# Hybrid encoder trunk: 64-row logit products padded to 128 rows, and dilated units that divide before they transpose

## The chip, the cores and the metric

The kernel runs on one core of one Trainium2 chip. The metric is the device time of one execution in microseconds (us). TensorE (PE below; PEld is its weight load) multiplies matrices, VectorE (DVE) and ScalarE (ACT) work on tiles of 128 partitions, GpSimd (POOL) does a few small powers, and SyncE (SP) issues the transfers.

## The reference

Input `x` is 512 positions by 1024 channels, float32; the output has the same shape. Two layers run, each on the residual `x`:

```
x = x + 1/2 * SwiGLU_1(rms(x))
u = rms(x);  p = u @ W_in
   A: Fourier mixing, 8 channel groups x 128
   B: dilated window attention, 3 head groups (dilation 1, 4, 16) x 2 heads of 64 channels;
      the groups of a head slot share one softmax denominator
   C: differential attention, 4 heads, two softmax maps of 64 channels each, a = p0 - lambda * p1
   a position bias is added to the logits of B and C
x = x + (sum over A, B, C of sigmoid gate * branch output) @ W_out
x = x + 1/2 * SwiGLU_2(rms(x))
```

A final RMSNorm follows. In B and C a logit is the product of a query and a key of 64 channels, scaled by 1/8, plus a bias; each row of logits goes through a softmax and is multiplied with the values.

## The kernel before, in words

**Number format.** Large products are made in parts. A float32 operand is split into `hi` (its float32r rounding, made by ACT) and `lo` (the remainder, made by DVE); `mm3` (line 186) makes a product as three passes, lo x hi, hi x lo and hi x hi. A pass is one weight load and one matmul of up to 128 rows (the channels that are summed over), 128 columns of weights and up to 512 columns of the moving operand. In the trace all passes have the line of the helper `mm` (183), so they are told apart by the names of their tiles; the engine helpers give DVE and ACT instructions line 124.

**Order of the work.** Each engine runs its instructions in program order. Weight chunks (`Op`, pushed to `ops`) are the dense work: load by SP, split by ACT and DVE, and some 24 passes each. Attention units are generators, the chains. `run` keeps two dilated or four differential units in flight; `step` advances a chain that is expected to be ready and otherwise emits the next step of dense work. What is expected is the `Estimate` (lines 94 to 127): each pass adds its given us to TensorE's time, each DVE and ACT instruction a fixed part and a part per column. Those figures decide the order of emission and nothing else.

**Logits.** `stack_query` (585) puts the hi part of a head's (or map's) 64 channels on its own half of the 128 rows and the lo part on the other half. `stack_key` (591) makes `kh`, the hi part of the key of both halves, and `k2`, in which map m has lo on its own half and hi on the other. `stacked` (601) then needs two passes instead of three: one of 128 rows, which holds both mixed products, and one of 64 rows, hi x hi:

```
        mm(ps, q2[:, m, cols], k2[:, m], True, False, 0.216)
        mm(ps, q2[HALF[m], m, cols], kh[HALF[m]], False, True, 0.216)
```

In the trace the first is `acc<-pr,pr 128*128 128x512` and the second `acc<-kh,pr 64*128 64x512`. A call of `stacked` is called a pair below.

**Dilated units** (`dilated_unit`, 733 on): 8 in a layer (2 head slots x 4 residues of the position). Each makes a pair for the first group, then two 64-row products in plain float32 of `q12` and `k12` for the other two groups (two passes each in the trace), a negated, biased minimum and the exponentials (`ta` of 512 columns, `tb_` of 256, with their sums), the sum's reciprocal `z`, and `dg`, the identity times `z` (line 756). Six products of 128x128 blocks with `dg` (lines 760 to 763) transpose and divide at once; in float32 each is two passes. The blocks are copied from PSUM and multiplied with the values.

**Differential units** (`diff_unit`): 16 in a layer (4 heads x 4 blocks of 128 queries). Each makes two pairs, one for each map; DVE takes bias and minimum (`mx`), ACT the exponential; DVE scales the first map by its reciprocal sum and adds the second (`ta<-ta,z,ta`). Four `T.transpose` with the identity (line 849) follow, one pass each, and after two blocks the product with the values.

**Between them.** After the Fourier groups, the dilated units are emitted among the products of the Fourier branch; the keys and queries of the differential heads follow, and the differential units run among the gate products and those of the dilated branch. PSUM has 8 tiles (`acc`) for everything; a tile is free again when DVE or ACT has read it. `kh` has two buffers.

Of the kernel before, what the change touches and what calls it, by code (L numbers as in the profile page):

```python
# [16 lines left out]
P = 128  # L17
# [18 lines left out]

# Columns of the one-hot tables: diff heads, dilation 1, 4, 16.
OH_DIFF, OH_D1, OH_D4, OH_D16, OH_N = 0, 1024, 2048, 2304, 2560
# [14 lines left out]
def _onehot():  # L53
    """[33, OH_N]: column -> one-hot bucket of a relative position; row 32 marks masked ones."""
    oh = np.zeros((BUCKETS + 1, OH_N), np.float32)

    def put(col, rel, valid):
        if valid:
            oh[int(_bucket(np.array(rel))), col] = 1.0
        else:  # L60
            oh[BUCKETS, col] = 1.0

    for i in range(1023):
        put(OH_DIFF + i, i - 511, True)
        put(OH_D1 + i, i - 511, abs(i - 511) <= 64)
    for i in range(255):
        put(OH_D4 + i, 4 * (i - 127), abs(i - 127) <= 64)
        put(OH_D16 + i, 4 * (i - 127), (i - 127) % 4 == 0)
    return oh


def _dft():
    """Channel table [128, C|S] with the scale of the transform, and position tables [2, 128, 512].

    Position table par acts on the sums (par 0) or negated differences (par 1) of the two halves of
    the positions; its 256 columns for each of two row blocks are cos and sin of output 2 j + par,
    j < 128. The column of sin 0 holds cos of output 256 instead."""
    c = np.arange(P)
# [15 lines left out]
class Estimate:  # L94
    """Expected times, in us, that choose the order of emission: `time` is TensorE's, `ready` that of
    the last result of the chain being emitted."""

# [11 lines left out]
class _Engine:  # L109
    """An engine whose instructions are added up in the estimate."""  # L110

# [18 lines left out]
def encoder_kernel(ctx: ExitStack, tc: tile.TileContext, I: dict, out: bass.AP):  # L130
# [13 lines left out]

# [1 line left out]
    # Engines run their instructions in program order. Latency-bound chains are generators; dense  # L146
    # matmul work is emitted between their steps, as much as they are expected to wait.
    est = Estimate()
# [37 lines left out]
    def mm3(ps, w, xx, start, stop, us=0.216):  # L186
        """ps += w.T @ xx of (hi, lo) pairs."""
        mm(ps, w[1], xx[0], start, False, us)
        mm(ps, w[0], xx[1], False, False, us)
        mm(ps, w[0], xx[0], False, stop, us)  # L190

    class Op:
        """A weight chunk and the generator that uses it."""

# [4 lines left out]
        def load(self, parts=1):  # L199
            """Loads part after part, then splits part after part."""  # L200
            n = self.nb * P
# [31 lines left out]
    def advance(c):  # L233
        """The next step of a chain; it yields the wait beyond its own last result."""
        est.ready = c[0]
        try:
            wait = next(c[1])
            c[0] = est.ready + wait
        except StopIteration:
            chains.remove(c)  # L240
# [52 lines left out]
    def project(ps, w, xs, k0=0, first=True, last=True):  # L293
        """ps (+)= sum over k of w[k].T @ xs[k], a step for each k"""
        for k in range(len(xs)):
            mm3(ps, wk(w, k0 + k), xs[k], first and k == 0, last and k == len(xs) - 1)
            yield

# [1 line left out]
    vecs = cpool.tile([P, I["vecs"].shape[1]], F32, name="vecs")  # L300
# [9 lines left out]
    halfb = cpool.tile([P, DEPTH * 24], F32, name="halfb")  # L310
    # Cosines of the channel transform, in float32.
    cosf = cpool.tile([P, P], F32, name="cosf")
# [5 lines left out]

# [1 line left out]
    def rstd_cols(sq, scale, eps, tag):  # L320
        """[128, 4] of (scale * column sums of sq + eps) ** -0.5 (column c: positions 128 c ...)."""
        ss = acc()
# [11 lines left out]
    def diagonals(cols):  # L334
        """The diagonal matrices of cols, in two parts."""
        n = cols.shape[1]
# [10 lines left out]
    def bcast(dg, n=NTB):  # L347
        """PSUM [128, n * 128]: every row is the column sums of dg."""
        ps = acc()
# [4 lines left out]
    class Norm:  # L354
        """rms statistics of x, gathered block by block, and x * gain as float32r pairs."""

# [40 lines left out]
        def then(self, act):  # L397
            """act() as soon as the statistics are there"""
            def wait():
# [9 lines left out]
    class LastNorm:  # L409
        """The last norm, with its output, for each half of the positions."""  # L410

# [29 lines left out]

# [1 line left out]
    def ffn(l, which, norm, nxt):  # L443
# [63 lines left out]

# [1 line left out]
    skewed = []  # L509

    def bias_tables():
# [13 lines left out]
        for head in range(10):  # L525
# [3 lines left out]
            sk = dram.tile([P, pitch], F32, name=f"skew{head}")  # L529
            # Row p of sk is the head's vector moved by step_ * p.  # L530
            nc.sync.dma_start(
# [5 lines left out]
    def toeplitz(dst, head, base, n):  # L537
        """dst[p, j] = bias vector of the head at base - step_ * p + j"""
        nc.sync.dma_start(dst, skewed[head][:, base:base + n])

# [1 line left out]
    def token_major(l, norm, name, n, evict):  # L542
        """u @ the n columns of a weight, rows on partitions: one PSUM tile for each 128 positions."""
        ps = []
# [21 lines left out]
    def feature_tile(l, norm, t, scale, use):  # L566
        """use(rows of u @ W_in's columns of tile t, times scale)"""
        def body(w):
# [11 lines left out]

    # Logits of 64 channels: both mixed products of the parts in one pass of 128 rows. Of the two
    # heads (or maps) of a tile, m sits on rows 64 m ...; its other part lies on the other half.
    HALF = (slice(0, 64), slice(64, 128))

    def stack_query(view, q2, src):
        for m in range(2):
            own, other = HALF[m], HALF[1 - m]
            A.activation(view(q2[own, m]), src[own], AF.Copy)
            V.tensor_tensor(view(q2[other, m]), src[own], view(f(q2[own, m])), op=ALU.subtract)

    def stack_key(src):
        kh = tpool.tile([P, 512], F32R, tag="kh", name=nm("kh"), bufs=2)
        k2 = pair()
        A.activation(kh, src, AF.Copy)
        for m in range(2):
            own, other = HALF[m], HALF[1 - m]
            V.tensor_tensor(k2[own, m], src[own], f(kh[own]), op=ALU.subtract)
            A.activation(k2[other, m], src[own], AF.Copy)
        return kh, k2

    def stacked(ps, q2, cols, key, m):
        kh, k2 = key
        mm(ps, q2[:, m, cols], k2[:, m], True, False, 0.216)
        mm(ps, q2[HALF[m], m, cols], kh[HALF[m]], False, True, 0.216)

    def by4(ap):
        return ap.rearrange("p (u r) -> p r u", r=4)

    # Fourier mixing. The position transform of real rows gives cosine and sine sums, which are even
    # and odd in the output position s: Y[k, s] = P - Q and Y[k, 512 - s] = P + Q with  # L610
    # P = C Zcos, Q = S Zsin.
    def fourier_tables():
# [13 lines left out]
    def fold(norm, eo):  # L626
        """Sums and negated differences of the two halves of the positions."""
        def evict(ps):
# [46 lines left out]

    # Dilated attention: a joint softmax over the three groups of a head slot, for the queries of
    # one residue mod 4. The first group sees all keys (masked), the others those of the residue.
    def dilated_inputs(l, norm):
# [54 lines left out]
    def dilated_unit(d, po, s, r, bias):  # L733
# [20 lines left out]
        V.reciprocal(z, z)  # L754
        dg = spool.tile([P, P], F32, tag="dg", name=nm("dg"), bufs=2)
        V.tensor_scalar(dg, ident, z, None, op0=ALU.mult)
        yield 0.1
        # Transposes that divide by the sum.
        qa, qb_ = acc(), acc()
        for c in range(4):  # L760
            mm(qa[:, c * P:(c + 1) * P], ta[:, c * P:(c + 1) * P], dg, True, True, 0.216)
        for g in range(2):
            mm(qb_[:, g * P:(g + 1) * P], tb_[:, g * P:(g + 1) * P], dg, True, True, 0.216)
        pa, pb = tma(), tma()
# [7 lines left out]

    # Differential attention.
    def diff_inputs(l, norm):
        lam_init = 0.8 - 0.6 * math.exp(-0.3 * l)
        d = {"vc": [], "y": [None] * NDIFF}
        # -lambda on every partition
        lq = tma()
# [106 lines left out]
    def gate(l, norm, b, o, use):  # L885
        """use(tanh of half the gate's argument): 2 sigmoid(z) = 1 + tanh(z / 2)"""
        def body(w):
# [11 lines left out]
    def branch(src, nb, ys, use):  # L899
        """use(branch output)"""  # L900
        def body(w):
# [152 lines left out]
def _tiles(w):  # L1054
    """[L, K, N] -> [L, N/128, 128, K]: for each 128 columns, rows of 128 by row blocks."""
    L, K, N = w.shape
    return w.reshape(L, K // P, P, N // P, P).transpose(0, 3, 2, 1, 4).reshape(L, N // P, P, K)
# [54 lines left out]
```

## Time and profile before

| | |
|---|---|
| time, median of 3 runs | 2505.75 us (2504.47 to 2506.02) |
| span of the profiled execution | 2505.5 us |
| mean granted TensorE clock | 0.996 of full speed |
| PE / PEld busy | 2486.9 / 2051.9 us |
| DVE / ACT / POOL busy | 1263.0 / 900.9 / 16.4 us |
| DMA | 241.06 MB, 96 GB/s on average |

The profile is of one execution; the runs were timed separately, and no other time is given for the profiled one than its span, from the first to the last instruction. A matmul's end is modelled and passes overlap, so the distance from one start to the next, not the duration, tells what a pass costs. `xN` is the number of instructions that a row stands for. "issue" as the end of an idle time means that the engine waited for nothing that the profile shows.

### The profile page before, as it was taken

How to read it: one execution, taken by the hardware profiler on the slowest of the kernel's cores; microseconds unless marked ns; L12 is line 12 of the kernel's file. 1: busy time of each engine (PE TensorE's matmuls, PEld its weight loads, DVE VectorE, ACT ScalarE, POOL GpSimd, SP SyncE). 2: the span in 40 equal slices, each digit the busy share in tenths (PEclk: the TensorE clock that was granted, in tenths of full speed). 3: DMA queues.
4: the chain of work that ended last, by engine and by line, in shares of the span. 5: the costliest groups of instructions: out<-in, count | busy, mean ns of one | idle time of the engine just before them, and what ended most of it. 6: DMA issues, size and time to landing. Idle time of an engine off the chain costs nothing.

```text
span 2505.5 us, 28932 instructions
## 1 busy us (share of the span) xinstructions
PE 2486.9 (99%) x11618; PEld 2051.9 (82%) x11618; DVE 1263.0 (50%) x1961; ACT 900.9 (36%) x1335; POOL 16.4 (1%) x20
## 2 busy tenths in 40 slices
PE   8999999999999999999999999999999999999998
PEld 6788889887778888888888888888877788888888
DVE  5434454534775654344444344445367656443446
ACT  4222233534443332223332233344344444322234
POOL 0000000000000000000000000000000000000000
PEclk9999999999999999999999999999999999999999
DMA  4533232312222322332332323333122223223335
GB/s 155 154 93 106 91 101 93 96 57 75 94 72 81 115 93 90 96 104 88 103 101 80 114 93 88 100 100 98 50 85 77 79 71 114 93 85 109 99 95 160
DMA packets 82486, 241.06 MB, mean 96 GB/s; under 512 B 9305, under 2 KB 17241, under 8 KB 82352
## 3 DMA queue, kind: packets, MB, share of 16 engines
q1 hardware_dynamic: 82352, 239.22, 31.2%
q8 instruction: 91, 1.49, 0.2%
q14 instruction: 43, 0.35, 0.0%
HBM read 235.93 MB, written 6.91 MB: 97 GB/s over the span
## 4 chain that ended last, share of the span: by engine, by line
PE 99%; DVE 0%; DMA 0%; ACT 0%; issue 0%; POOL 0%; SPq 0%; POOLq 0%; DVEq 0%
PE acc L183 98%; PE acc L849 1%; DMA x<-in_xT 0%; DVE pr L124 0%; POOL srr L124 0%; ACT xs L124 0%; DVE xs L124 0%; DMA out<-t 0%; DVE t L124 0%; DVE wlo L124 0%; DVE sum L124 0%; SPq L1017 0%; SPq L205 0%; POOLq L1107 0%; ACT ch L124 0%
## 5 line engine op out<-in xcount | busy, mean ns | idle before, releaser
L183 PE MATMUL acc<-xs,whi 128*128 128x512 f32 x4032 | 1246.9, 390 | 0.3 <-DVE xs L124 0.3
L124 ACT ACTIVATE whi<-raw 128x1024 fp32r<-128x1024 f32 (+3 forms) x495 | 463.2, 936 | 1244.8 <-PE acc L183 740.7
L183 PEld LDWEIGHTS acc<-xs,whi 128*128 128x128 f32 x4032 | 759.1, 188 | 158.3 <-DVE xs L124 1.7
L183 PE MATMUL acc<-xs,wlo 128*128 128x512 f32 x2016 | 794.1, 394 | 7.4 <-ACT xs L124 5.7
L124 DVE TENSOR_TENSOR wlo<-raw,whi 128x1024 fp32r<-128x1024 f32 (+3 forms) x495 | 528.6, 1068 | 372.9 <-ACT whi L124 371.4
L183 PE MATMUL acc<-pr,whi 128*128 128x512 f32 (+1 forms) x2256 | 650.3, 373 | 0.0
L183 PEld LDWEIGHTS acc<-pr,whi 128*128 128x128 f32 x2256 | 412.1, 188 | 74.1 <-DVE pr L124 0.5
L183 PEld LDWEIGHTS acc<-xs,wlo 128*128 128x128 f32 x2016 | 379.9, 188 | 95.2 <-issue 9.6
L183 PE MATMUL acc<-pr,wlo 128*128 128x512 f32 (+1 forms) x1128 | 422.6, 375 | 0.0
L124 DVE TENSOR_TENSOR t<-acc,rows 128x512 f32<-128x512 f32 x238 | 163.8, 691 | 507.6 <-PE acc L183 505.5
L183 PEld LDWEIGHTS acc<-pr,wlo 128*128 128x128 f32 x1128 | 212.4, 188 | 38.1 <-issue 0.3
L183 PE MATMUL acc<-whi,xs 128*128 128x512 f32 (+1 forms) x512 | 153.6, 376 | 0.0
L124 ACT ACTIVATE pr<-t 128x512 fp32r<-128x512 f32 (+2 forms) x152 | 101.8, 670 | 56.3 <-DVE t L124 55.7
L124 DVE SCALAR_TENSOR_TENSOR x<-acc,x 128x512 f32<-128x512 f32 (+1 forms) x88 | 56.6, 643 | 127.2 <-PE acc L183 127.2
L183 PE MATMUL acc<-pr,pr 128*128 128x256 f32 (+2 forms) x624 | 112.8, 310 | 0.0
L183 PEld LDWEIGHTS acc<-whi,xs 128*128 128x128 f32 x512 | 95.3, 188 | 15.0
L183 PEld LDWEIGHTS acc<-pr,pr 128*128 128x128 f32 (+1 forms) x624 | 86.3, 190 | 17.6 <-issue 9.9
L183 PE MATMUL acc<-wlo,xs 128*128 128x512 f32 (+1 forms) x256 | 96.1, 375 | 0.0
L124 DVE TENSOR_TENSOR pr<-t,pr 128x512 fp32r<-128x512 f32 (+1 forms) x124 | 86.4, 697 | 6.2 <-ACT pr L124 5.6
L124 ACT ACTIVATE pr<-acc 128x512 fp32r<-128x512 f32 (+1 forms) x66 | 39.7, 608 | 80.4 <-PE acc L183 56.0
L124 DVE CUSTOM_DVE_ANT_0 ta<-acc,pr 128x512 f32<-128x512 f32 x80 | 54.4, 689 | 28.1 <-PE acc L183 27.4
L124 DVE TENSOR_TENSOR t<-t,t 128x512 f32<-128x512 f32 x88 | 60.9, 692 | 10.2 <-ACT t L124 1.3
(90 smaller groups left out, 1028.5 us busy)
## 6 DMA issues: line engine op xcount, KB each, us to landing
raw<-in_w_ffn_up SPq DMA_DIRECT2D x88, 512.0 KB
raw<-in_w_ffn_gate SPq DMA_DIRECT2D x87, 512.0 KB
raw<-in_w_ffn_down SPq DMA_DIRECT2D x72, 384.0 KB
raw<-in_w_gate SPq DMA_DIRECT2D x48, 512.0 KB
raw<-in_w_ffn_down SPq DMA_DIRECT2D x72, 320.0 KB
raw<-in_w_in SPq DMA_DIRECT2D x28, 512.0 KB
raw<-in_w_a SPq DMA_DIRECT2D x16, 512.0 KB
raw<-in_w_br_a SPq DMA_DIRECT2D x16, 512.0 KB
```

Source lines behind the costliest of these rows:

```text
L124: return call(out, *args, **kwargs)
L183: T.matmul(ps, w, xx, start=start, stop=stop)
L849: T.transpose(tr[:, c * P:(c + 1) * P], es[0][:, c * P:(c + 1) * P], ident)
```

## The change

The second pass of a pair takes all 128 rows. Two key tiles `kz`, made once, hold for each map the hi part on its own half of the rows and zeros on the other; the zeros are written by POOL at the start, and `stack_key` writes only the own halves, for each map with a copy of 64 rows. The weights of the pass are the whole of `q2[:, m]`, whose other half meets the zeros. The estimate of both passes goes from 0.216 to 0.228.

In a dilated unit DVE multiplies `ta` and `tb_` with `z` in place, and six transposes with the identity take the place of the six products with `dg`; their estimate goes from 0.216 to 0.109 each.

The program's scratch for dynamic DMA is made smaller. Comments and docstrings go as well, which moves no instruction.

```
--- before.py
+++ after.py
@@ -588,27 +588,37 @@
             A.activation(view(q2[own, m]), src[own], AF.Copy)
             V.tensor_tensor(view(q2[other, m]), src[own], view(f(q2[own, m])), op=ALU.subtract)
 
+    kzs = deque()
+    for i in range(2):
+        kz = cpool.tile([P, 2, 512], F32R, name=f"kz{i}")
+        for m in range(2):
+            nc.gpsimd.memset(f(kz[HALF[1 - m], m]), 0.0)
+        kzs.append(kz)
+
     def stack_key(src):
-        kh = tpool.tile([P, 512], F32R, tag="kh", name=nm("kh"), bufs=2)
+        kz = kzs[0]
+        kzs.rotate(1)
         k2 = pair()
-        A.activation(kh, src, AF.Copy)
         for m in range(2):
             own, other = HALF[m], HALF[1 - m]
-            V.tensor_tensor(k2[own, m], src[own], f(kh[own]), op=ALU.subtract)
+            A.activation(kz[own, m], src[own], AF.Copy)
+            V.tensor_tensor(k2[own, m], src[own], f(kz[own, m]), op=ALU.subtract)
             A.activation(k2[other, m], src[own], AF.Copy)
-        return kh, k2
+        return kz, k2
 
     def stacked(ps, q2, cols, key, m):
-        kh, k2 = key
-        mm(ps, q2[:, m, cols], k2[:, m], True, False, 0.216)
-        mm(ps, q2[HALF[m], m, cols], kh[HALF[m]], False, True, 0.216)
+        kz, k2 = key
+        mm(ps, q2[:, m, cols], k2[:, m], True, False, 0.228)
+        mm(ps, q2[:, m, cols], kz[:, m], False, True, 0.228)
 
@@ -752,15 +762,16 @@
         z = small(1, "z")
         V.tensor_add(z, s2[:, 0:1], s2[:, 1:2])
         V.reciprocal(z, z)
-        dg = spool.tile([P, P], F32, tag="dg", name=nm("dg"), bufs=2)
-        V.tensor_scalar(dg, ident, z, None, op0=ALU.mult)
+        V.tensor_scalar(ta, ta, z, None, op0=ALU.mult)
+        V.tensor_scalar(tb_[:, :256], tb_[:, :256], z, None, op0=ALU.mult)
         yield 0.1
         qa, qb_ = acc(), acc()
         for c in range(4):
-            mm(qa[:, c * P:(c + 1) * P], ta[:, c * P:(c + 1) * P], dg, True, True, 0.216)
+            T.transpose(qa[:, c * P:(c + 1) * P], ta[:, c * P:(c + 1) * P], ident)
+            est.pe(0.109)
         for g in range(2):
-            mm(qb_[:, g * P:(g + 1) * P], tb_[:, g * P:(g + 1) * P], dg, True, True, 0.216)
+            T.transpose(qb_[:, g * P:(g + 1) * P], tb_[:, g * P:(g + 1) * P], ident)
+            est.pe(0.109)
         pa, pb = tma(), tma()
         A.activation(pa, qa, AF.Copy)
         V.tensor_copy(pb[:, :256], qb_[:, :256])
@@ -1098,7 +1109,7 @@
-    nc = bacc.Bacc("TRN2", target_bir_lowering=False, num_devices=1)
+    nc = bacc.Bacc("TRN2", target_bir_lowering=False, num_devices=1, dynamic_dma_scratch_size=1024)
```

## Rows read from the trace of the kernel before

**Rows 1.** The page's busy line: us, share of the span and instructions of each engine.

```profile
PE 2486.9 (99%) x11618; PEld 2051.9 (82%) x11618; DVE 1263.0 (50%) x1961; ACT 900.9 (36%) x1335; POOL 16.4 (1%) x20
```

**Rows 2.** Groups by shape: count | busy us, mean ns of one | idle before, releasers.

```profile
L183 PE MATMUL acc<-kh,pr 64*128 64x512 f32 x80 | 41.5, 519 | 0.0
...
L183 PE MATMUL acc<-dg,ta 128*128 128x128 f32 x192 | 24.3, 278 | 0.0
...
L124 DVE TENSOR_SCALAR ta<-ta,z 128x512 f32<-128x512 f32 x32 | 15.3, 480 | 0.0
L183 PEld LDWEIGHTS acc<-kh,pr 64*128 64x128 f32 x80 | 15.2, 190 | 21.8 <-issue 21.8
...
L124 ACT ACTIVATE pr<-t 64x512 fp32r<-64x512 f32 x40 | 27.1, 676 | 0.6
...
L124 DVE TENSOR_SCALAR dg<-ident,z 128x128 f32<-128x128 f32 x16 | 4.6, 287 | 0.5
```

**Rows 3.** Timeline of PE, 606 to 620: start us, us, engine, line, operation, names, shape, count.

```profile
606.01 0.39 PE L183 MATMUL acc<-xs,wlo 128*128 128x512 f32 x1
...
608.05 0.39 PE L183 MATMUL acc<-pr,pr 128*128 128x512 f32 x1
608.37 0.50 PE L183 MATMUL acc<-kh,pr 64*128 64x512 f32 x1
...
612.22 0.58 PE L183 MATMUL acc<-pr,pr 128*128 128x512 f32 x1
...
616.35 0.79 PE L183 MATMUL acc<-xs,wlo 128*128 128x512 f32 x1
...
619.43 0.63 PE L183 MATMUL acc<-xs,whi 128*128 128x512 f32 x2
```

**Rows 4.** Stretches: bounds and length, busy us (instructions) of each engine, PEclk, DMA share, GB/s.

```profile
612.50:619.30 6.80, 6.80 (x13) 3.80 (x13) 4.72 (x17) 4.41 (x11) 0.00 (x0) 0.50 0.00 0
619.30:710.00 90.70, 90.70 (x416) 70.77 (x415) 65.93 (x126) 41.19 (x73) 1.01 (x1) 1.00 0.26 83
1848.00:1855.00 7.00, 7.00 (x14) 3.82 (x14) 4.68 (x17) 4.63 (x11) 0.00 (x0) 0.51 0.00 0
```

**Rows 5.** Timeline of PE, 64 to 70, the bias tables' products.

```profile
65.75 0.61 PE L183 MATMUL acc<-xs,whi 128*128 128x512 f32 x2
66.30 1.02 PE L183 MATMUL acc<-ta,rel 33*10 33x512 f32 x2
```

**Rows 6.** Timeline of PE, 547 to 549, a dilated unit's logits.

```profile
547.52 0.50 PE L183 MATMUL acc<-pr,pr 128*128 128x512 f32 x1
547.95 0.49 PE L183 MATMUL acc<-kh,pr 64*128 64x512 f32 x1
548.29 0.60 PE L183 MATMUL acc<-pr,pr 64*128 64x128 f32 x4
```

**Rows 7.** Timeline of PE, 508 to 518 and 630 to 632, transposes.

```profile
511.01 2.84 PE L183 MATMUL acc<-dg,ta 128*128 128x128 f32 x24
...
513.92 0.63 PE L183 MATMUL acc<-pr,whi 128*128 128x512 f32 x2
...
630.80 0.60 PE L849 MATMUL acc<-ident,ta 128*128 128x128 f32 x4
...
631.47 0.63 PE L183 MATMUL acc<-xs,whi 128*128 128x512 f32 x2
```

**Rows 8.** Timeline of DVE, 606 to 622, two of the differential units' reductions.

```profile
608.91 0.69 DVE L124 CUSTOM_DVE_ANT_0 ta<-acc,pr 128x512 f32<-128x512 f32 x1
...
609.75 0.69 DVE L124 CUSTOM_DVE_ANT_0 ta<-acc,pr 128x512 f32<-128x512 f32 x1
```

**Rows 9.** Waits of PE's weight loads: us in total, times, longest us.

```profile
PEld acc L183 <- DVE mx L124: 1.5, 6, 0.2
```

**Rows 10.** Timeline of all engines, 547 to 553: a diagonal and the transposes that use it.

```profile
550.12 0.29 DVE L124 TENSOR_SCALAR dg<-ident,z 128x128 f32<-128x128 f32 x1
...
550.99 1.50 PE L183 MATMUL acc<-dg,ta 128*128 128x128 f32 x12
```

## The prediction

> **What bounds the kernel now.** I read the page's busy line first: TensorE (PE) is busy 99% of the span, VectorE (DVE) 50%, ScalarE (ACT) 36% [rows 1]. So only time on PE's own queue counts, and the question is which of its steps are longer than they need be. A start-to-start step is what a pass costs; durations overlap and mislead. The groups by shape gave the candidates: 80 passes named `acc<-kh,pr` of 64 rows, before each of which the weight load sat idle for "issue" [rows 2]. The PE timeline prices them: the nine steps of ordinary 128-row passes from 606.01 to 608.05 take 0.227 us each, but from 608.37 on, where passes of 128 and of 64 rows alternate, the nine steps to 612.22 take 0.428 us each [rows 3]. Nothing else was waited for. The same pause stands where a 33-row pass of the bias tables follows a 128-row one: 66.30 is 0.32 us after the pass before it (the second of the pair that starts at 65.75), not 0.227 [rows 5]. So the height of the pass is the cause, not the operand: going from one height to another, the next weights are not loaded ahead. Last, the stretches: from 612.5 to 619.3 and around 1850 the granted clock is 0.50 (1.2 GHz), elsewhere here 1.00 (2.4 GHz) [rows 4]. The first begins about 4 us into the longest alternating run of its layer (eight pairs, from 608.05) [rows 3]; the second lies in the same place of the other layer.
>
> **The change part by part.** All sums are against the profiled execution; its span is 2505.5 us, and the runs' median is 2505.75, so 0.25 lies around it and no correction is made. A measurement of this kernel can tell about 0.2% (5 us) from no change.
>
> *Differential logits.* Of the 80 pairs, 16 belong to dilated units (two layers of eight) and 64 to the differential heads (two layers of 4 x 4 x 2). In the timeline the 64 stand in 20 runs of 2, 4 or 8 pairs. The first step of a run is 0.32 (608.05 to 608.37), the others 0.428 [rows 3]: 20 x 0.32 + 108 x 0.428 = 52.6 us. The pass that follows a run has its own weights late and is followed after 0.34 instead of 0.227 (the like: 547.95 to 548.29 [rows 6]): 20 x 0.11 = 2.2. Padded to 128 rows, all 128 passes are ordinary ones, 128 x 0.227 = 29.1, since no step in the trace depends on the values. **Saved: 52.6 + 2.2 - 29.1 = 25.7 us.**
>
> *The two stretches at half clock.* From 612.22 to 619.43 took 7.21 us [rows 3]. In it lie six alternating steps (to 616.35), the step that follows the run (0.34) and six ordinary ones; at full clock 6 x 0.428 + 0.34 + 6 x 0.227 = 4.27. So a stretch costs 2.94 us. What PE did before the clock fell was the alternating run; without pauses that run is like the thousands of passes around it, at clock 1.00. I take both stretches as gone. **Saved: 5.9 us**; bound the other way, nothing.
>
> *Dilated logits.* Here the 64-row products of the other two groups (`q12`, `k12`) stay, so the change of height only moves: from before `kh` to after it. Before, 0.43 (547.52 to 547.95) and then 0.34 to the first q12 pass [rows 6], or 0.32 and 0.34 where the run begins with its weights loaded. After: 0.227 and 0.32 (the price in rows 5). That is 0.11 to 0.22 a unit; the middle, 0.165 x 16. **Saved: 2.6 us** (1.8 to 3.5).
>
> *Dilated transposes.* A product with the diagonal is two passes: 192 records for 96 blocks [rows 2]. Between 511.01 and 513.92 lie 24 of them and one ordinary pass: (2.91 - 0.227) / 24 = 0.112 a pass, 0.224 a block [rows 7]. The differential units already transpose with the identity: four blocks and one ordinary pass from 630.80 to 631.47, (0.67 - 0.227) / 4 = 0.111 a block, one pass each [rows 7]. **Saved: 96 x 0.113 = 10.8 us.** The clock stays at 1.00 from 619.3 to 710, a stretch with such transposes in it [rows 4]; but they come four at a time there, and six or twelve in the dilated units. The Trainium skill, "TensorE: Matmul & The Clock Gate", Part 4, says that passes in transpose mode do not count as activity for the clock gate. By that rule dilated stretches could fall to half clock, and the sum would lose what the last rival below gives; by the row it loses nothing.
>
> *Division on VectorE.* A unit loses the diagonal (0.287 us) and gains a scaling of 512 columns (0.480) [rows 2] and one of 256 (between these two, about 0.35): 0.54 us more, 8.7 us over 16 units, on an engine half idle. It sits between the reciprocal and the transposes, so it delays them; what is queued behind it on DVE are the weight splits of the branch products that fill PE meanwhile. The least cover in the trace is 0.58 us: the diagonal is there at 550.41, PE takes it at 550.99 [rows 10]; the other units have more. The emission order is chosen by the kernel's own estimate, which charged 0.20 for the diagonal and charges 0.94 for the two scalings, so filler is placed ahead of the transposes for more than the 0.54 added. Cost 0; with that cover gone, up to 8.7.
>
> *Keys.* A key copies two halves of 64 rows (0.676 each [rows 2]) instead of all rows at once, on ACT: at most 0.68 more for each of 10 keys, hidden under the passes of the following weight chunk. Cost 0; cover gone, 6.8.
>
> *Rings, memsets, scratch.* Two fixed key tiles in turn are as many as the two rotating ones. The four POOL memsets come once at the start; POOL has 16.4 us of work in all [rows 1] and the first key needs them only after the first FFN and projections. All transfers are issued by SP, none by POOL, so the smaller scratch touches none. Cost 0 each. The altered estimates (0.228 for 0.216, 0.109 for 0.216) shift the order of filler: nothing is added to PE, and I allow 3 us either way.
>
> *What is late next.* PE now makes a map's logits in 0.454 us, while DVE takes 0.84 to reduce one (608.91 to 609.75) [rows 8]. Before, the pair's 0.856 just matched it. Eight PSUM tiles take up the difference in the short runs, but not wholly: PE's weight loads already waited six times, 1.5 us in all, for a reduction (`mx`) to free its tile [rows 9]. I charge one pair's gain, 0.4, for each: **2.4 us given back** (0, if eight tiles are enough, to 4.8, if twice as many maps wait).
>
> Sum: 25.7 + 5.9 + 2.6 + 10.8 = 45.0, less 2.4: 42.6 us. 2505.5 - 42.6 = **2463 us**.
>
> **The rivals.**
> - *The clock still falls in the long runs*: the padded passes carry zeros and the two stretches stay. Against: what precedes the fall is alternation alone, never plain passes. 2463 + 5.9 = 2469.
> - *The chains become the bound*: every map waits for DVE's 0.84, and the dilated transposes for their scaling. For: DVE is busy 65.93 of 90.70 us from 619.3 to 710 [rows 4], and its in-order queue also holds the weight splits. Against: the first transposes come at 630.80, 14 us after the run's last logits at 616.35 [rows 3, 7], so there is filler to absorb it. It gives back the 25.7 (less the 2.4 charged) and 8.7: 2463 + 23.3 + 8.7 = 2495.
> - *The padding does nothing*: if the pause came from the parts (hi after lo) and not from the height, the padded pass would pause too. Against: the 33-row passes [rows 5]. Only the transposes are gained: 2505.5 - 10.8 = 2495.
> - *Slower: the clock in the dilated phase*. Twelve or six transposes in a row, beside 64-column products, let the clock fall in each of the 14 groups (seven a layer; the first is that of 511.01), and the two old stretches stay: 16 x 2.94 = 47.0, so 2463 + 47 = 2510. It decides from 15 stretches on (42.6 / 2.94 = 14.5); with fewer the kernel is still faster. Against: a group of twelve takes 1.3 us amid dense passes, and no such stretch is seen around the transposes there are [rows 4].
>
> **How the numbers follow.** Forecast 0.78; clock stays 0.08; chains 0.07; padding without effect 0.03; clock in the dilated phase 0.03. The likeliest gives 2463. Low end: no tile waits (-2.4), the better end of the dilated logits (-0.9), order in our favour (-3): 2457. High end: the clock stretches stay (+5.9), twice the tile waits (+2.4), half of the dilated scaling exposed (+4.3): 2476. That leaves out the two cases near 2495 and the slower one, 0.13 together, and a little of the forecast's edges. Only the last rival is not faster by over 5 us: with 13 to 16 stretches it is no change or slower, and I split its 0.03 so; a further 0.01 covers what I haven't thought of. So faster 0.96, same 0.02, slower 0.02.
>
> **What would show it.** Right: passes of `kz` at steps of 0.227 and the idle "issue" before their weight loads gone in the differential heads, but still one before the q12 passes; clock 1.00 through both long runs; 224 passes with the identity where 128 were, and no `dg`; DVE scaling 512 columns 48 times and 256 columns 16 times; PE still at 99%. Wrong: waits of PE for `mx` growing in number and length, PE idle before transposes for a scaling, new stretches at clock 0.50 near the dilated groups, or 0.43 steps at `kz`.

## The result, and the profile after

| | before | after |
|---|---|---|
| time, median | 2505.11 us (2503.92 to 2506.02, 4 runs) | 2465.80 us (2465.05 to 2467.14, 4 runs) |
| ratio of the times, 95% interval | | 0.9841 (0.9827 to 0.9855) |
| span of the profiled execution | 2505.5 us | 2464.0 us |
| the two token-mixing stretches | 318.70 + 318.71 us | 297.11 + 297.17 us |
| all the rest of the span | 1868.1 us | 1869.7 us |

The kernel is 1.6% faster; 2463 us was forecast, 2457 to 2476 the range. A mixing stretch is counted here from the first 64-row (later `kz`) pass of a layer to the norm's broadcast ahead of the merged output. All of the gain lies in these two, 21.6 and 21.5 us. They differ by 43.1 us, the medians by 39.3; the part on the total says why.

The page's busy line after: TensorE is still the bound, and has 41.6 us less to do.

```profile
PE 2445.3 (99%) x11522; PEld 2037.4 (83%) x11522; DVE 1265.9 (51%) x1977; ACT 902.0 (37%) x1345; POOL 19.5 (1%) x24
```

The groups by shape after (count | busy us, mean ns | idle before). The 21.8 us that the weight loads of the hi x hi passes sat idle [rows 2] are 2.1 now. The 192 passes with the diagonal are 96 with the identity (64 and 32), and VectorE scales 512 columns 48 times and 256 columns 16 times:

```profile
L183 PE MATMUL acc<-kz,pr 128*128 128x512 f32 x80 | 31.4, 393 | 0.0
...
L124 DVE TENSOR_SCALAR ta<-ta,z 128x512 f32<-128x512 f32 x48 | 23.2, 483 | 0.6
...
L183 PEld LDWEIGHTS acc<-kz,pr 128*128 128x128 f32 x80 | 15.1, 189 | 2.1
...
L770 PE MATMUL acc<-ident,ta 128*128 128x128 f32 x64 | 9.6, 272 | 0.0
...
L773 PE MATMUL acc<-ident,ta 128*128 128x128 f32 x32 | 6.1, 273 | 0.0
...
L124 DVE TENSOR_SCALAR ta<-ta,z 128x256 f32<-128x256 f32 x16 | 5.6, 348 | 0.0
```

The PE timeline where the long run of the differential units stands now (before: [rows 3]). The steps are 0.227 to 0.23 us, `pr` or `kz` alike: 14 passes from 604.29 to 607.48 take 3.19 us. VectorE takes the first of these maps only at 607.65, 2.7 us after its last pass, since a weight split and two 64-row remainders stand ahead in its queue. The eighth pair waits for the tile that this reduction frees (0.69 us instead of 0.227, and 0.34 to the pass behind it). PE's rows, then VectorE's:

```profile
604.29 0.39 PE L183 MATMUL acc<-pr,pr 128*128 128x512 f32 x1
604.52 0.39 PE L183 MATMUL acc<-kz,pr 128*128 128x512 f32 x1
...
607.48 0.39 PE L183 MATMUL acc<-xs,wlo 128*128 128x512 f32 x1
607.71 0.40 PE L183 MATMUL acc<-xs,whi 128*128 128x512 f32 x1
608.40 0.50 PE L183 MATMUL acc<-pr,pr 128*128 128x512 f32 x1 [0.30 <-DVE mx L124]
608.74 0.39 PE L183 MATMUL acc<-kz,pr 128*128 128x512 f32 x1
```

```profile
606.21 1.40 DVE L124 TENSOR_TENSOR pr<-t,pr 64x512 fp32r<-64x512 f32 x2
607.65 0.69 DVE L124 CUSTOM_DVE_ANT_0 ta<-acc,pr 128x512 f32<-128x512 f32 x1
...
608.26 0.69 DVE L124 CUSTOM_DVE_ANT_0 ta<-acc,pr 128x512 f32<-128x512 f32 x1
```

Stretches of the kernel after (columns as in [rows 4]; the clock is the third number from the end): the long runs and the dilated phases of both layers.

```profile
604.30:607.50 3.20, 3.20 (x16) 2.64 (x15) 2.69 (x4) 1.77 (x3) 0.00 (x0) 1.00 0.17 24
607.50:710.00 102.50, 102.20 (x494) 85.26 (x493) 80.00 (x167) 55.08 (x105) 1.01 (x1) 1.00 0.26 82
493.00:570.00 77.00, 77.00 (x405) 61.02 (x404) 32.45 (x83) 30.19 (x59) 0.00 (x0) 1.00 0.24 74
1707.00:1785.00 78.00, 78.00 (x410) 61.82 (x410) 33.28 (x84) 30.20 (x59) 0.00 (x0) 1.00 0.23 73
1818.60:1821.80 3.20, 3.20 (x16) 2.64 (x15) 2.69 (x4) 1.71 (x3) 0.00 (x0) 1.00 0.21 26
```

The clock is 1.00 in all five. So both stretches at half clock are gone, and the transposes, six in a row, bring no new ones. The Trainium skill ("TensorE: Matmul & The Clock Gate", Part 4) says that a transpose doesn't count as a busy TensorE in the same way as other passes; in these dilated stretches the clock stayed at 1.00 with them.

The waits of PE and of its weight loads for a reduction to free a PSUM tile (us, times, longest), in place of six [rows 9]: both lines are the same two places, one in each layer.

```profile
PE acc L183 <- DVE mx L124: 0.6, 2, 0.3
```

```profile
PEld acc L183 <- DVE mx L124: 1.5, 2, 0.7
```

### The profile page after: what moved, and what is told of

It is laid out like the page before. It is cut to its first block, busy times and chain, and to the rows that moved or that the text cites. A ratio compares the mean times of both kernels' runs of the same rounds, so it can differ in the third digit from the quotient of the medians.

```text
span 2464.0 us, 28761 instructions
## 1 busy us (share of the span) xinstructions
PE 2445.3 (99%) x11522; PEld 2037.4 (83%) x11522; DVE 1265.9 (51%) x1977; ACT 902.0 (37%) x1345; POOL 19.5 (1%) x24
## 4 chain that ended last, share of the span: by engine, by line
PE 98%; DMA 1%; DVE 1%; ACT 0%; issue 0%; SPq 0%; POOL 0%; POOLq 0%; DVEq 0%; ACTq 0%
PE acc L183 97%; PE acc L860 1%; PE acc L770 0%; DMA raw<-in_w_ffn_down 0%; DMA x<-in_xT 0%; DMA out<-t 0%; DVE wlo L124 0%; PE acc L773 0%; DVE pr L124 0%; POOL srr L124 0%; ACT xs L124 0%; DVE t L124 0%; DVE xs L124 0%; ACT whi L124 0%; DVE sum L124 0%
```

## The experiments

The theory: a pass whose height (rows of the array) differs from that of the pass before it can't have its weights loaded ahead, which costs about 0.1 to 0.2 us at each change; a long run of such changes also lets the clock fall. Padding takes away the changes; the transposes take one pass out of two. The rivals: the pause follows the parts (hi after lo) or the data type; the zeros matter; VectorE's part shows; the order of emission makes the difference. Mixing stretches are given as the first layer's and the second's, counted as above, from each kernel's trace.

**The padding alone.**

```
-        V.tensor_scalar(ta, ta, z, ...); V.tensor_scalar(tb_[:, :256], ...)
+        V.tensor_scalar(dg, ident, z, None, op0=ALU.mult)
-            T.transpose(qa[...], ta[...], ident)
+            mm(qa[...], ta[...], dg, True, True, 0.216)
```

> The padding alone; dilated units keep the products with the diagonal. If the terms of the sum add up: 2505 less 25.7 (differential pairs), 5.9 (two half-clock stretches), 2.6 (dilated pairs), plus 2.4 of tile waits: about 2473 us, clock 1.00 through both long runs. If the padding does nothing and the transposes carry the gain: about 2505. If the transposes are worth nothing: 2466, as the full change.

2476.23 us (2475.33 to 2477.51), ratio 0.9881 (0.9868 to 0.9895). Mixing 302.53 + 302.91: 32.0 us less than before, where 25.7 + 5.9 + 2.6 - 2.4 = 31.8 was forecast; by the times it is 30.7 (the kernel before took 2506.93 us beside it). The stretches of its two long runs, both at clock 1.00:

```profile
609.80:616.00 6.20, 5.90 (x26) 4.57 (x25) 5.65 (x13) 3.90 (x10) 0.00 (x0) 1.00 0.26 86
1829.60:1836.00 6.40, 5.82 (x26) 4.46 (x25) 5.58 (x13) 4.09 (x10) 0.00 (x0) 1.00 0.25 83
```

**The transposes and the division alone** (the other half of the diff, on the kernel before).

> The dilated transposes and the division on VectorE alone; the 64-row passes stay. Theory: 96 blocks at 0.111 instead of 0.224 us, so 10.8 us less, about 2494, and both stretches at half clock still there. Rival, the scaling is exposed: 16 x 0.54 of it comes back, about 2503. Rival, transposes let the clock fall: new stretches at clock 0.50 in the dilated phases, 2.94 us each, 2497 and more.

2496.55 us (2491.77 to 2497.61), ratio 0.9959 (0.9946 to 0.9971). Mixing 312.67 + 312.58: 12.2 us less than before; against the padding alone, the full change has 11.2 less. By the times it is 10.4 us (the kernel before took 2506.93 beside it), and 10.9 from the padding alone to the change with ones, below; so it isn't clear that 10.8 was low. The parts add up: 32.0 + 12.2 = 44.2 by mixing, the full change 43.1. The time lies near the last rival's 2497, so it is the clock that tells the two apart: the stretches of the long runs are still at half clock, and the first layer's dilated phase (third row) is at full, as is the second layer's.

```profile
608.90:615.70 6.80, 6.80 (x14) 4.22 (x14) 5.08 (x18) 3.88 (x9) 0.00 (x0) 0.50 0.00 0
1837.70:1844.50 6.80, 6.80 (x13) 3.63 (x13) 4.24 (x17) 4.70 (x11) 0.00 (x0) 0.50 0.00 0
493.00:570.00 77.00, 77.00 (x407) 61.81 (x406) 32.23 (x82) 29.96 (x59) 0.00 (x0) 1.00 0.23 74
```

**Ones instead of zeros.**

```
-            nc.gpsimd.memset(f(kz[HALF[1 - m], m]), 0.0)
+            nc.gpsimd.memset(f(kz[HALF[1 - m], m]), 1.0)
```

> The change, but the padding half of the key tile holds ones instead of zeros, so a logit also gets the sum of the query's other half added. Theory: what counts is the height of the pass, so the same time as the change, 2464 to 2468, and the same clock. Rival, the zeros spare or cost the clock something: a difference of at least one stretch, 3 us, or another granted clock in the two long runs.

2465.37 us (2465.22 to 2466.56); mixing 297.10 + 297.17, the change's own to 0.01 us. The zeros are neither a saving nor a burden.

**The q12 products padded too** (`k12z` holds zeros on the other half, as `kz` does; its zeros and the key's copies by halves are left out here).

```
+    k12z = cpool.tile([P, 2, 2, 512], F32, name="k12z")
...
-            mm(lb[...], q12[sl, g, rs], k12[sl, g, rs], True, True, 0.216)
+            mm(lb[...], q12[:, g, rs], k12z[:, s, g, rs], True, True, 0.216)
```

> The change, and the 64-row float32 products of q12 and k12 padded with zeros as well, so that no 64-row pass is left. Theory (a change of height costs a pause each way): per dilated unit 0.33 becomes 0.227 before the first of them, 0.20 becomes 0.11 after the last, and the pass after that is followed after 0.227 instead of 0.34: 0.30 x 16 = 4.8 us less than the change, about 2461. Rival, the pause belongs to the hi and lo parts or to float32r next to float32: no gain, 2466.

2459.31 us (2458.03 to 2460.79), ratio 0.9812 (0.9798 to 0.9825); 6.1 us less than the change with ones, which ran beside it. Mixing 293.82 + 293.84: 6.6 us less than the change. So these float32 passes cost their height too, and a little more than forecast. The first dilated unit of the change, then of this kernel (start us, us): before the q12 products 0.33 has become 0.24.

```profile
493.03 0.39 PE L183 MATMUL acc<-pr,pr 128*128 128x512 f32 x1
493.26 0.40 PE L183 MATMUL acc<-kz,pr 128*128 128x512 f32 x1
493.59 0.48 PE L183 MATMUL acc<-pr,pr 64*128 64x128 f32 x2
```

```profile
493.48 0.39 PE L183 MATMUL acc<-pr,pr 128*128 128x512 f32 x1
493.70 0.39 PE L183 MATMUL acc<-kz,pr 128*128 128x512 f32 x1
493.94 0.38 PE L183 MATMUL acc<-k12z,pr 128*128 128x128 f32 x2
494.08 0.48 PE L183 MATMUL acc<-pr,pr 128*128 128x512 f32 x1
```

**A shorter run, no padding.**

```
-UNITS_IN_FLIGHT = 4
+UNITS_IN_FLIGHT = 2
```

> The kernel before with two differential units in flight instead of four, so that the longest alternating run is four pairs, not eight. Theory: the clock falls because of the long alternating run; with runs of four it stays at 1.00 and the two stretches, 2.94 us each, are gone: 5.9 us less than before. Rival, the clock falls for another reason (the start of the phase): no gain, stretches at 0.50 still there. If two in flight don't cover the chains, PE waits before transposes and it is slower than before.

2514.79 us (2514.10 to 2517.12), ratio 1.0039 (1.0025 to 1.0053): slower, as the last case foresaw, so the time tells nothing of the clock, but the stretches do. The run, now four pairs, is at 1.00. At the end of the phase, where no filler is left and PE waits for the chains, the clock now falls:

```profile
608.00:612.00 4.00, 4.00 (x12) 1.89 (x11) 3.18 (x8) 3.55 (x7) 0.00 (x0) 1.00 0.04 14
798.10:804.80 6.70, 6.70 (x22) 4.87 (x23) 4.94 (x13) 2.78 (x7) 0.00 (x0) 0.50 0.08 22
2033.70:2043.80 10.10, 9.86 (x34) 7.38 (x34) 6.74 (x18) 3.17 (x8) 1.38 (x1) 0.50 0.00 0
```

So the start of the phase doesn't let the clock fall there: with a run of half the length it stays up. The new falls come among alternating pairs too, the first layer's right behind 2.5 us of PE waits and two groups of four transposes, the second layer's within a wait of 1.97 us; which of these they follow stays open.

**The same passes, grouped by height** (kernel before).

```
-            lg = acc()
-            stacked(lg, qp, bs, kp, m)
+        lgs = [acc(), acc()]
+        for m in range(2):
+            mm(lgs[m], qp[:, m, bs], kp[1][:, m], True, False, 0.216)
+        for m in range(2):
+            mm(lgs[m], qp[HALF[m], m, bs], kp[0][HALF[m]], False, True, 0.216)
...
```

> The kernel before with the four passes of a differential unit in another order: both 128-row passes, then both 64-row ones. Same passes, same operands, half the changes of height. Theory: a unit's 4 x 0.428 = 1.71 us becomes 0.43 + 0.34 + 0.32 + 0.34 = 1.43, or about 1.2 if the two 64-row passes, on different halves of the rows, overlap: 0.28 to 0.5 x 32 = 9 to 16 us less than before, with no padding at all. Rival, the pause follows from hi after lo or from the count of passes: the same as before. The Trainium skill, TensorE: Matmul & The Clock Gate, Part 3, would have the two halves run side by side.

2488.97 us (2487.59 to 2490.13), ratio 0.9932 (0.9919 to 0.9944): 16.9 us less with the same 64-row passes, a little over the 9 to 16 forecast. The order of the parts changes here with that of the heights, so this run alone doesn't end the rival of the parts. The padded kernels do: they keep the parts in the old order, at steps of 0.227 us. Its PE timeline at the start of the run:

```profile
609.29 0.61 PE L183 MATMUL acc<-pr,pr 128*128 128x512 f32 x2
609.84 0.50 PE L183 MATMUL acc<-kh,pr 64*128 64x512 f32 x2
610.27 0.74 PE L183 MATMUL acc<-pr,pr 128*128 128x512 f32 x2
...
611.36 0.73 PE L183 MATMUL acc<-pr,pr 128*128 128x512 f32 x2
```

Two 64-row passes together, from 609.84 to 610.27, take 0.43 us, what one alone took, and are busy for 0.50 us in all, as one was [rows 3]: on different halves of the array they run side by side. The Trainium skill ("TensorE: Matmul & The Clock Gate", Part 3) states that overlap, and this trace agrees. A unit takes 1.09 us (610.27 to 611.36), against 1.71 before and 0.91 padded. By the unit, (1.71 - 1.09) x 32 = 19.8 us and the old half-clock stretches were to be gained; mixing is 308.62 + 308.67, 20.1 less. The clock now falls for 3.4 us at the end of each phase, where PE waits for ScalarE (`ta`, 1.4 us in two places) and for VectorE (`pr`, 0.8 in two). As an estimate, two falls at 1.36 us (the price of the next experiment) and these waits give back 4.9 of the 19.8 + 5.4, which leaves 20.3.

**The smaller scratch alone.**

```
-    nc = bacc.Bacc("TRN2", target_bir_lowering=False, num_devices=1)
+    nc = bacc.Bacc("TRN2", target_bir_lowering=False, num_devices=1, dynamic_dma_scratch_size=1024)
```

> The kernel before with the smaller scratch for dynamic DMA alone. Theory: no transfer uses it, the same as before within 2 us. Rival: transfers wait longer, slower than before.

2506.73 us (2504.27 to 2509.27), ratio 1.0003 (0.9994 to 1.0012): nothing. Its trace happens to price the clock: in layer 1 the half-clock stretch lasts 3.4 us instead of 6.8, and mixing takes 317.25 us there and 318.61 in layer 2. The 3.4 us at half clock cost 1.36 us, so 6.8 cost about 2.7 by estimate; 2.94 was forecast. Its windows around the two:

```profile
615.80:619.10 3.30, 3.30 (x7) 2.09 (x7) 2.63 (x10) 2.73 (x7) 0.00 (x0) 0.50 0.00 0
1848.00:1854.70 6.70, 6.70 (x12) 3.49 (x12) 4.07 (x16) 4.51 (x12) 0.00 (x0) 0.50 0.00 0
```

**The change with the old estimates** (0.216 for 0.228 and for 0.109).

> The change with the old figures in the estimate (0.216 for a padded pass and for a transpose), so that only the order of emission differs from the change. Theory: filler moves, nothing is added to PE: the same as the change, 2464 to 2468, at most 3 us off. Rival, the order holds part of the gain: slower than the change by more than 3 us, with PE waiting for VectorE.

2465.77 us (2465.03 to 2466.92); mixing 297.59 + 297.59, 0.45 us a layer more than the change. The order holds next to nothing of the gain.

**The division doubled.**

```
+        nc.vector.tensor_scalar(ta, ta, 1.0, None, op0=ALU.mult)
+        nc.vector.tensor_scalar(tb_[:, :256], tb_[:, :256], 1.0, None, op0=ALU.mult)
         V.tensor_scalar(ta, ta, z, None, op0=ALU.mult)
```

> The change with the scalings of the dilated units doubled: each of ta and tb is multiplied by 1 first, outside the estimate, so that the order is the change's: 0.48 + 0.35 = 0.83 us more of VectorE in a unit's chain. Theory, the division is hidden (least cover in the change's trace 1.55 us): the same time as the change within 1 us. Rival, VectorE's part of the chain shows: up to 16 x 0.83 = 13 us slower than the change.

2464.02 us (2463.37 to 2466.98); mixing 297.09 + 297.12: the same. But the trace shows that it doubled less than meant. The two extra scalings took 0.423 and 0.287 us, and the first ran while VectorE still waited for ScalarE's last sum, ahead of `z`:

```profile
540.07 0.43 DVE L765 TENSOR_SCALAR ta<-ta 128x512 f32<-128x512 f32 x1 [0.88 <-ACT ta L124]
540.56 0.16 DVE L124 TENSOR_TENSOR z<-s 128x1 f32<-128x1 f32 x1
```

In this unit, the one with the least cover, the time from the last scaling to the transposes only fell from 1.55 to 1.48 us, and in no unit by more than 0.41, so the run tests little. That the division itself is hidden is read from the change's trace: no wait of PE for a scaling is in it, and the least cover has grown from 0.58 us [rows 10] to 1.55. The estimate's higher charge for the scalings would explain that; it wasn't tried alone. A unit's second scaling ends at 543.46, its transposes begin at 545.01 (the change, all engines):

```profile
542.71 0.75 DVE L124 TENSOR_SCALAR ta<-ta,z 128x512 f32<-128x512 f32 x2
...
545.01 0.60 PE L770 MATMUL acc<-ident,ta 128*128 128x128 f32 x4
```

**A version that beats both: the columns as well.** On the kernel with q12 padded:

```
-            mm(po[sl, rs], v0[:, c, sl], pa[...], c == 0, False, 0.108)
+            mm(po[s][:, rs], v0[:, c, :], pa[...], c == 0, False, 0.108)
...
```

> The kernel with q12 and k12 padded, and in the dilated units also the products with the values at the full width: 128 columns of weights (both head slots) instead of 64, the half that isn't wanted left unused, and one PSUM tile for each slot. Theory: a change of the columns pauses PE as one of the rows does (in the change's trace 0.32 instead of 0.227 before such a group, 0.20 instead of 0.11 after it, 0.34 instead of 0.227 one pass later): 0.30 x 16 = 4.8 us less than with q12 padded alone, about 2454.5. Rival, the second PSUM tile makes PE wait or the wider weight loads show: no gain, 2459 or more.

> The change itself again, on the chip of its neighbours in this call: 2465 to 2467.

2455.69 us (2454.46 to 2456.41), ratio 0.9794 (0.9781 to 0.9807). The change again, on the same chip: 2465.51 us (2463.46 to 2466.74), ratio 0.9833 (0.9820 to 0.9846). So the wider columns and the padded q12 together take 9.8 us off the change. Mixing is 292.03 + 292.04: 3.6 us of it from the columns, where 4.8 was forecast. A group of 12 value products, 64 columns wide in the change and 128 here (start us, us), takes 1.45 and 1.26 us until the next pass:

```profile
533.05 1.52 PE L183 MATMUL acc<-ta,pr 128*64 128x128 f32 x12
534.50 0.50 PE L183 MATMUL acc<-pr,pr 128*128 128x512 f32 x1
```

```profile
529.70 1.50 PE L183 MATMUL acc<-ta,pr 128*128 128x128 f32 x12
530.96 0.48 PE L183 MATMUL acc<-pr,pr 128*128 128x512 f32 x1
```

## Why the prediction was right

*What bounds the kernel*: right. PE is busy 99% before and after, and the gain is the time taken off its queue. One support was weaker than I took it for: the 33-row pass [rows 5] also has only 10 columns of weights, and a change of columns alone pauses PE too, as the last experiment shows. That row couldn't tell the two apart; the padded kernels do.

*Differential and dilated logits, and the clock* (25.7 + 2.6 + 5.9, less 2.4 = 31.8): right; the padding alone gives 32.0. Two sizes were off in opposite directions (5.4 for 5.9, and in the full change 1.2 for 2.4), and with them the terms give 32.5, so the fit to 0.2 us is partly luck. That the height is the cause is shown by the padded passes, which take 0.227 us with the same parts in the same order, and from three more sides: grouping the same passes gains, padding the float32 products gains again, and the padding's values don't matter. The stretches at half clock are gone, as forecast; the shorter run keeps the clock up at its place, and a stretch is priced at about 2.7 us, not 2.94.

*Dilated transposes* (10.8): right, measured 11.2 by mixing with the padding and 12.2 without, 10.9 and 10.4 by the times. Six blocks and one ordinary pass of the change stand from 513.75 to 514.64, (0.89 - 0.227) / 6 = 0.11 us a block, where a block with the diagonal took 0.224 [rows 7]:

```profile
513.75 0.60 PE L770 MATMUL acc<-ident,ta 128*128 128x128 f32 x4
514.18 0.38 PE L773 MATMUL acc<-ident,ta 128*128 128x128 f32 x2
514.32 0.48 PE L183 MATMUL acc<-pr,wlo 128*128 128x512 f32 x1
514.64 0.62 PE L183 MATMUL acc<-pr,whi 128*128 128x512 f32 x2
```

*Division, keys, memsets, scratch, estimates* (0): right for the scratch and the estimates, each tried alone. For the division the trace shows cover, which the doubling hardly tested. Keys and memsets weren't tried alone; no wait of PE for either is among those of the change.

*What is late next* (2.4): the place was right, the size too high. PE waits once in each layer, behind the long run: (0.69 - 0.227) + (0.34 - 0.227) = 0.58 us, 1.2 in all. The working had a wrong price: the 0.84 us from one reduction to the next [rows 8] is not what VectorE takes for a map. The second map's last pass began at 609.22 and ran 0.49 us, so its reduction couldn't start before 609.71; VectorE was waiting for PE:

```profile
609.22 0.49 PE L183 MATMUL acc<-kh,pr 64*128 64x512 f32 x1
```

Where the logits are there, as in the change, the next reduction starts after 0.61 us (607.65 to 608.26). So the wait comes less from VectorE's rate than from its late start behind the split and the remainders, and the rival in which every map waits for 0.84 stood on a figure that was too high. Eight tiles do carry the short runs, and VectorE is busy 80.0 of 102.5 us from 607.5 to 710 without holding PE up elsewhere there.

*The total*: the steps said 42.6 us, the mixing stretches show 43.1 (2 x 318.7 less 297.11 and 297.17). The forecast of 2463 is 2.8 us low for two reasons outside the sum. First, I took 0.25 us to lie around the span. The change's profiled execution took 2466.0 us with a span of 2464.0, and a later run of the kernel before 2508.58 with 2506.8: some 2 us lie around it, and the profiled execution of before was simply slower than the median. Second, in the profiled execution of the change the clock fell to 0.50 for 3.4 us at the end of a wait of PE of 1.76 us in the first FFN, which adds 1.3 us ahead of the mixing; before had the same wait without the fall, and so had the change when it ran again. This fall and the slow profiled execution of before are also why the medians differ by 39.3 us only; when the change ran again beside the kernel before, they differed by 42.1. The first window is the change's, the second that of its second run:

```profile
16.70:20.10 3.40, 3.22 (x8) 2.55 (x9) 3.29 (x6) 2.51 (x4) 0.00 (x0) 0.50 0.52 165
```

```profile
16.70:20.10 3.40, 2.80 (x12) 2.35 (x13) 3.30 (x5) 2.94 (x5) 0.00 (x0) 1.00 0.49 148
```

## What to carry to other kernels

On a TensorE-bound kernel, price passes by start-to-start steps for each pair of neighbours: a shape that differs from its neighbours' in rows or columns can cost more than the rows it saves, and here padding with zeros to the common shape was worth 32 us of logits and, carried through, 10 more. If small passes must stay, put those of one height together, on different halves of the array. A float32 product whose only job is to transpose is two passes where a transpose is one; a division folded into it is cheaper on an engine with time to spare.

## What was not expected

Two neighbouring 64-row passes on the two halves took 0.43 us together, as much as one, so grouping alone gave 0.9932 (0.9919 to 0.9944) without any padding. The fall of the clock needs no wait of PE: in the kernel before, PE was busy all through the 7.5 us ahead of it (ends of passes are modelled), the later part of them a run of alternating heights:

```profile
605.00:612.50 7.50, 7.50 (x26) 4.36 (x24) 4.97 (x13) 4.84 (x11) 0.00 (x0) 1.00 0.24 71
```

And the same idle time at the head of the program let the clock fall in some executions and not in others, which moves the time by 1.3 us.
